# Products of the recurrent half's output projection issued one by one instead of in groups

## The chip, the cores and the metric

The kernel runs on one core of one Trainium2 chip. The metric is the device time of one execution in microseconds (us); lower is better. The engines are named as in the profile: PE is TensorE (matmuls), PEld its weight loads, DVE is VectorE, ACT is ScalarE, POOL is GpSimd, SP is SyncE, which issues all transfers here. Every engine works through its own queue strictly in program order and waits on semaphores for the others.

## The reference, cut to what matters

Two layers run over 512 tokens of width 1024. Layer 1 has a recurrent mixer (a diagonal state-space part and a gated DeltaNet of 6 heads) and then a convolutional FFN. The change lies where layer 1's mixer ends and its FFN begins.

```python
def recurrent_mixer(h, w_in, ...):
    u, q, k, v, z, a, beta_raw = split_cols(h @ w_in, REC_SPLITS)
    yc = s5_mixer(u, ...)                                  # 256 columns
    yd = gated_deltanet_mixer(q, k, v, z, a, beta_raw, ...)  # 6 heads x 128
    return jnp.concatenate([yc, yd], axis=-1) @ w_out      # the output projection

x = x + g1 * recurrent_mixer(modulate(x, norm_mix, sh1, sc1), ...)
h = modulate(x, norm_ffn, sh2, sc2)                        # RMS norm, scale, shift
x = x + g2 * conv_ffn(h, w_up, conv_w, w_down)
```

The delta rule solves a triangular system per chunk and head, then steps through the chunks with a state S that each chunk hands to the next.

## The kernel before

Everything is stored transposed: 8 tiles of 128 channels x 512 tokens. A float32 product is made from three passes (`mm3`): each operand is split into a high and a low part (`hh`/`hl` for activations, `whi`/`wlo` for weights), and high x high, high x low and low x high are accumulated in one PSUM bank. In the trace these are rows of L393 and L394.

**Weights.** `prep` loads a 512 KB weight tile (`st`), ScalarE casts it to `whi` (L363) and VectorE subtracts to make `wlo` (L364). There are two `st` buffers and five `whi`/`wlo` pairs, so a later tile's cast waits until an earlier product has let its pair go.

**The solve and scan.** The DeltaNet heads go in pairs (0, 1, 2). For each pair, `levels` inverts the triangular blocks in small matmuls (L1356, L1363, L1374, L1381, L1384, L1393, L1398, in this order) with a VectorE or ScalarE copy between any two of them. `scan` then makes four chunk steps for both heads: W times the right side (L1414), the state update (L1421), the next chunk's right side (L1409) and the outputs (L1429, L1430), again each waiting for a copy. After the last step come squares on ScalarE (L1443), an inverse root on VectorE (L421 to L426), the gated output `vs` (L1450), eight transposes (L1453) and a copy (L1456), whose result is split into the last two of the eight operand pairs of the output projection (`REC_K` puts them at the end of its sum).

**The output projection.** `out_gemm` makes 8 output tiles m. Tiles 0 to 3 go to the banks acc, acc, t and x over all 512 tokens, as 24 products each of 128x512. For tiles 0 and 1 the last of the eight operand pairs is a part of its own. Tiles 4 to 7 go to s, s, o and o in two halves of 256 tokens, 24 products of 128x256 for each tile and half. After each half of the tokens `norm` follows: a sum over channels (L520), an inverse root on VectorE (L421 to L426), its spread over partitions (L530), and `make_h` (L549 to L551), which writes that half of the FFN's input. The FFN's first four up products also run half by half; then come its tiles in o, o, t and x, and from L626 on the fast scheme `seven`.

**What sets the order.** The program is written once, and a list scheduler lays out each engine's queue before the run, by priorities that follow the written order; work whose inputs are late falls behind ready work. `gemm` hands its products to `runs`, which cuts them into groups of 12 (24 for the 256-token halves). What `together` does with a group depends on one flag:

```python
if not self.grouped:
    for c in calls:
        c()
    return
first = calls[0]()
with self.tc.issue_after(first.ins), self.tc.high_priority(offset=URGENT):
    for c in calls[1:]:
        c()
```

With the flag on, once the first product of a group is placed, the other 11 or 23 get a priority 4000 higher. The flag is off during the recurrent mixer itself and on elsewhere.

Of the kernel before, what the change touches and what calls it, by code (L numbers as in the profile page):

```python
# [249 lines left out]
class Kernel:  # L250
# [887 lines left out]
    def recurrent(self):  # L1138
# [456 lines left out]
        for n in REC_K[len(SPLIT_AT):]:  # L1595
            self.split(Y[n], *rhs[n], half=n < 2)
        self.close("rt")
        self.grouped = True
        self.xp = self.open("x2", "right")
        self.x = [self.xp.tile([P, T], F32, name=f"x{k}") for k in range(KD)]  # L1600
        for k in range(KD):
# [2 lines left out]
        self.keep, self.keep_pool = {}, self.open("fg1", "right")  # L1604
        self.out_gemm([("ro", m) for m in range(8)], rhs, lambda m: self.gate(1, 0, m), 1, 1, hC, REC_K, ("acc", "acc", "t", "x", "s", "s", "o", "o"))
        self.close("hB")

    def build(self):
        nc, I = self.nc, self.I
# [87 lines left out]
```

## Time and profile before

| | us |
|---|---|
| median of 3 runs | 1303.36 |
| the runs | 1301.78, 1303.36, 1312.18 |
| profiled execution, its own time | 1304.43 |
| its span, first to last instruction | 1302.6 |
| PE busy in the span | 1269.6 (97%) |
| DVE busy | 1006.7 (77%) |
| ACT busy | 632.1 (49%) |

A busy PE here is one with a matmul in flight, at whatever clock. The time outside the span is 1.8 us. The stretch that the change touches lies between 868 us, where the solve of pair 2 begins, and 1016 us, a little into the FFN of layer 1.

### The profile page before, as it was taken

What the parts mean: (1) busy time and instruction counts of PE and PEld (TensorE: products, weight loads), DVE (VectorE), ACT (ScalarE), POOL (GpSimd) and SP (SyncE); (2) the same over time, 40 slices, a digit from 0 to 9 for tenths busy, and PEclk for the clock granted to TensorE, in tenths of its full rate; (3) what the DMA queues carried; (4) which work ended last, traced back from release to release, by engine and by line L of the source; (5) the groups of instructions that cost most, each with busy time, mean ns of one, the idle gap of its engine ahead of it and who ended that gap; (6) DMA issues with size and microseconds to landing.
All of it is one profiled execution on the core that took longest, in us unless ns stands there. A gap on an engine that the chain in (4) does not pass through costs nothing.

```text
span 1302.6 us, 22709 instructions
## 1 busy us (share of the span) xinstructions
PE 1269.6 (97%) x8814; PEld 1084.2 (83%) x8814; DVE 1006.7 (77%) x2195; ACT 632.1 (49%) x1214; POOL 12.5 (1%) x43
## 2 busy tenths in 40 slices
PE   8999999999999999999999999998899999999998
PEld 5988776998888888788988878786888999998998
DVE  6868886779995996696779686763679999888883
ACT  4466655445422432243374656552455656554550
POOL 0001000000000000000000000000000000000000
PEclk9999999999999999999999999999999999999999
DMA  9624544516664765473325332220412333332222
GB/s 367 227 84 151 180 153 147 207 46 232 209 198 166 241 227 198 130 239 133 126 102 155 121 97 59 85 62 13 169 47 98 105 102 102 102 102 100 96 84 103
DMA packets 83132, 181.14 MB, mean 139 GB/s; under 512 B 28560, under 2 KB 36176, under 8 KB 83024
## 3 DMA queue, kind: packets, MB, share of 16 engines
q1 hardware_dynamic: 83024, 179.69, 41.1%
q8 instruction: 69, 1.13, 0.4%
q14 instruction: 39, 0.32, 0.1%
HBM read 165.55 MB, written 14.11 MB: 138 GB/s over the span
## 4 chain that ended last, share of the span: by engine, by line
PE 80%; DVE 12%; ACT 4%; DMA 2%; issue 2%; SPq 0%; DVEq 0%; ACTq 0%
PE acc L393 20%; PE acc L394 10%; PE s L393 9%; PE o L393 8%; PE s L394 4%; PE o L394 4%; PE s L626 3%; PE o L626 3%; PE acc L626 2%; PE s L806 2%; PE o L841 1%; DVE wlo L364 1%; DMA st<-up 1%; PE x L393 1%; DVE wlo L332 1%
## 5 line engine op out<-in xcount | busy, mean ns | idle before, releaser
L363 ACT CAST whi<-st 128x1024 fp32r<-128x1024 f32 (+3 forms) x168 | 165.2, 986 | 217.0 <-PE acc L393 68.1
L364 DVE TENSOR_TENSOR wlo<-st,whi 128x1024 fp32r<-128x1024 f32 (+3 forms) x168 | 191.2, 1140 | 47.1 <-ACT whi L363 45.4
L393 PE MATMUL acc<-hh,whi 128*128 128x512 f32 (+1 forms) x392 | 141.5, 368 | 4.2 <-ACT hh L550 3.9
L393 PE MATMUL acc<-hl,whi 128*128 128x512 f32 (+1 forms) x392 | 141.3, 364 | 0.2 <-DVE hl L414 0.2
L394 PE MATMUL acc<-hh,wlo 128*128 128x512 f32 (+1 forms) x392 | 141.2, 363 | 0.0
L465 DVE CUSTOM_DVE_ANT_0 adaj<-ast,cond 128x1024 bf16<-128x1024 f32 x86 | 104.8, 1218 | 10.4 <-DMA ast<-ada 10.2
L393 PE MATMUL acc<-whi,hh 128*128 128x256 f32 x320 | 92.9, 291 | 0.4 <-ACT hh L550 0.4
L394 PE MATMUL acc<-whi,hl 128*128 128x256 f32 x320 | 90.4, 283 | 0.9 <-DVE hl L551 0.9
L393 PE MATMUL acc<-wlo,hh 128*128 128x256 f32 x320 | 90.4, 283 | 0.0
L393 PEld LDWEIGHTS acc<-hh,whi 128*128 128x128 f32 x392 | 73.4, 190 | 17.1 <-ACT hh L550 4.6
L393 PE MATMUL s<-hl,whi 128*128 128x512 f32 (+2 forms) x256 | 86.3, 340 | 0.0
L393 PE MATMUL s<-hh,whi 128*128 128x512 f32 (+2 forms) x256 | 85.8, 344 | 0.0
L393 PEld LDWEIGHTS acc<-hl,whi 128*128 128x128 f32 x392 | 74.0, 190 | 12.3 <-DVE hl L414 0.8
L394 PEld LDWEIGHTS acc<-hh,wlo 128*128 128x128 f32 x392 | 74.3, 190 | 11.1
L394 PE MATMUL s<-hh,wlo 128*128 128x512 f32 (+2 forms) x256 | 82.2, 339 | 0.0
L331 ACT CAST whi<-st 128x1024 fp32r<-128x1024 f32 x54 | 56.3, 1048 | 27.4 <-DVE st L340 7.8
L393 PE MATMUL o<-hh,whi 128*128 128x512 f32 (+1 forms) x192 | 68.8, 358 | 0.0
L332 DVE TENSOR_TENSOR wlo<-st,whi 128x1024 fp32r<-128x1024 f32 x54 | 65.5, 1216 | 4.1 <-ACT whi L331 4.1
L393 PE MATMUL o<-hl,whi 128*128 128x512 f32 (+1 forms) x192 | 68.5, 357 | 0.0
L394 PE MATMUL o<-hh,wlo 128*128 128x512 f32 (+1 forms) x192 | 68.5, 357 | 0.0
L393 PEld LDWEIGHTS acc<-whi,hh 128*128 128x128 f32 x320 | 60.2, 188 | 5.9 <-issue 4.0
L394 PEld LDWEIGHTS acc<-whi,hl 128*128 128x128 f32 x320 | 60.2, 188 | 1.9 <-DVE hl L551 1.5
(909 smaller groups left out, 3473.2 us busy)
## 6 DMA issues: line engine op xcount, KB each, us to landing
ast<-ada SPq DMA_DIRECT2D x92, 512.0 KB
st<-up SPq DMA_DIRECT2D x88, 512.0 KB
st<-ri SPq DMA_DIRECT2D x20, 512.0 KB
st<-wq SPq DMA_DIRECT2D x17, 512.0 KB
st<-dn SPq DMA_DIRECT2D x16, 448.0 KB
st<-dn SPq DMA_DIRECT2D x16, 384.0 KB
st<-dn SPq DMA_DIRECT2D x16, 320.0 KB
st<-wo SPq DMA_DIRECT2D x8, 512.0 KB
```

The costliest lines, as they stand in the source:

```text
L331: nc.scalar.copy(hi, src)
L332: nc.vector.tensor_tensor(lo, src, hi.bitcast(F32), ALU.subtract)
L363: nc.scalar.copy(hi, st)
L364: nc.vector.tensor_tensor(lo, st, hi.bitcast(F32), ALU.subtract)
L393: return [lambda: mm(out, lh, rh, start=start, stop=False), lambda: mm(out, lh, rl, start=False, stop=False), lambda: mm(out, ll, rh, star ...
L394: lambda: mm(out, ll, rh, start=False, stop=stop)]
L465: self.nc.vector.tensor_tensor_reduce(junk, st, self.cond, 1.0, 0.0, op0=ALU.mult, op1=ALU.add, accum_out=self.md[l][:, i:i + 1])
L626: nc.tensor.matmul(acc, x[:, s], y, start=start and k == n == 0, stop=k == 3 and n == 2, skip_group_check=not start)
L806: self.together([lambda sb=sb, pr=pr: nc.tensor.matmul(sb, qT[pr, i * P:(i + 1) * P], kT[pr, j0 * P:(i + 1) * P], start=True, stop=True) f ...
L841: calls.append(lambda j=j, par=par, vc=vc: nc.tensor.matmul(ob[64 * par:64 * par + 64, i * P:(i + 1) * P], V[:, j0 + j, vc:vc + 64], pts[: ...
```

## The change

The line that turns the flag on again moves from in front of the output projection to behind it. So the eight tiles' products, the last pair's solve and scan, and the two halves of the norm are all laid out with one product at a time to place. Nothing is added or removed; the same instructions run in another order.

```diff
         self.close("rt")
-        self.grouped = True
         self.xp = self.open("x2", "right")
 ...
         self.out_gemm([("ro", m) for m in range(8)], rhs, lambda m: self.gate(1, 0, m), 1, 1, hC, REC_K, ("acc", "acc", "t", "x", "s", "s", "o", "o"))
         self.close("hB")
+        self.grouped = True
```

The first place is TensorE in the solve of pair 2, from L1384 on. Names are out<-in with tile names; `acc` is tile 0 or 1 of the projection and `t` tile 2. Before:

```order
L1384 MATMUL s<-iW,z 32x32 x16
L393 MATMUL acc<-hh_9711,whi 128x512
L393 MATMUL acc<-hl_9712,whi 128x512
L394 MATMUL acc<-hh_9711,wlo 128x512
L393 MATMUL acc<-hh_9713,whi 128x512
L393 MATMUL acc<-hl_9714,whi 128x512
L394 MATMUL acc<-hh_9713,wlo 128x512
L1393 MATMUL s<-x_6823,nq 64x64 x8
```

With the change, TensorE at the same place:

```order
L1384 MATMUL s<-iW,z 32x32 x16
L393 MATMUL acc<-hh_9715,whi 128x512
L393 MATMUL acc<-hl_9716,whi 128x512
L394 MATMUL acc<-hh_9715,wlo 128x512
L1393 MATMUL s<-x_6823,nq 64x64 x8
L393 MATMUL acc<-hh_9717,whi 128x512
L393 MATMUL acc<-hl_9718,whi 128x512
L394 MATMUL acc<-hh_9717,wlo 128x512
L1398 MATMUL s<-wf,x_6823 64x64 x8
```

Three products stand between two steps of the solve where 6 or 12 stood.

The second place is TensorE at the end of pair 2's scan, where L1430 writes the last outputs and L1453 transposes the gated result. Before:

```order
L1421 MATMUL s<-vk,kt 128x128
L1430 MATMUL o<-vn,nq 128x128 x2
L1409 MATMUL s<-St,kT 128x128
L1429 MATMUL o<-St,qd 128x128
L1414 MATMUL s<-rh,wf 128x128
L1430 MATMUL o<-vn,nq 128x128
L1453 MATMUL s<-ident,vs 128x128 x7
L393 MATMUL s<-hh_9711,whi 128x256
L393 MATMUL s<-hl_9712,whi 128x256
```

With the change, TensorE from the last L1414 on:

```order
L1414 MATMUL s<-rh,wf 128x128
L393 MATMUL t<-hl_9716,whi 128x512
L1430 MATMUL o<-vn,nq 128x128
L394 MATMUL t<-hh_9715,wlo 128x512
L1430 MATMUL o<-vn,nq 128x128
L393 MATMUL t<-hh_9717,whi 128x512
L393 MATMUL t<-hl_9718,whi 128x512
L394 MATMUL t<-hh_9717,wlo 128x512
```

Behind the last L1430 now stand 19 products of tiles 2 and 3 (t and x) before the first L1453, and single products between the transposes; before, nothing stood between the two.

The third place is TensorE around the first half's norm, where L520 sums over channels and L530 spreads the inverse root. Before:

```order
L393 MATMUL o<-hl_9726,whi 128x256
L394 MATMUL o<-hh_9725,wlo 128x256
L530 MATMUL t<-ident,nry 128x128 x2
L520 MATMUL x<-ones,stat 128x1 x2
L393 MATMUL acc<-hh_10048,whi 128x256 x2
L393 MATMUL s<-hh_10048,whi 128x256 x2
```

With the change, TensorE around the same L530:

```order
L393 MATMUL s<-hh_9723,whi 128x256
L393 MATMUL s<-hl_9724,whi 128x256
L530 MATMUL t<-ident,nry 128x128 x2
L394 MATMUL s<-hh_9723,wlo 128x256
L393 MATMUL s<-hh_9725,whi 128x256
L393 MATMUL s<-hl_9726,whi 128x256
```

The first L530 used to stand behind the whole projection; now 52 of its products, all of the second half of the tokens, stand behind it and 31 between it and its L520. The second half's L520 and L530 stand 48 and 72 products into the FFN's first up products, where before the first half's L530 and the second half's L520 stood next to each other.

## Rows read from the trace of the kernel before

**Rows 1.** Busy time by stretch: from:to, length, busy us of each engine, PEclk, DMA.

```profile
846.00:860.00 14.00, 14.00 (x115) 13.32 (x114) 10.70 (x39) 5.81 (x20) 0.00 (x0) 1.00 0.30 65
...
903.00:910.00 7.00, 2.82 (x10) 1.87 (x11) 4.20 (x21) 2.15 (x10) 0.00 (x0) 0.75 0.00 0
910.00:914.00 4.00, 4.00 (x12) 3.14 (x12) 0.69 (x1) 0.29 (x1) 0.00 (x0) 0.59 0.88 266
...
947.00:951.00 4.00, 4.00 (x22) 3.90 (x21) 4.00 (x11) 1.90 (x5) 0.00 (x0) 0.57 0.49 186
...
963.00:995.00 32.00, 32.00 (x185) 28.09 (x184) 31.18 (x57) 22.65 (x38) 0.00 (x0) 1.00 0.15 50
```

**Rows 2.** Timeline of PE, pair 1: start, us, instruction, idle before and releaser.

```profile
837.58 0.69 PE L1374 MATMUL s<-iX,nq 32*32 32x32 f32 x32
...
845.88 0.38 PE L1414 MATMUL s<-vs,wf 128*128 128x128 f32 x2
...
848.04 0.39 PE L1409 MATMUL s<-St,kT 128*128 128x128 f32 x2
```

**Rows 3.** Timeline of PE, pair 2: solve and scan.

```profile
868.33 0.75 PE L1356 MATMUL s<-iX,nq 32*32 32x32 f32 x64
...
875.37 0.69 PE L1374 MATMUL s<-iX,nq 32*32 32x32 f32 x32
...
888.24 0.61 PE L1414 MATMUL s<-vs,wf 128*128 128x128 f32 x4
...
892.37 0.39 PE L1409 MATMUL s<-St,kT 128*128 128x128 f32 x2
...
893.27 0.43 PE L1414 MATMUL s<-rh,wf 128*128 128x128 f32 x2
...
894.92 0.38 PE L1421 MATMUL s<-vk,kt 128*128 128x128 f32 x2
...
903.09 0.49 PE L1430 MATMUL o<-vn,nq 128*128 128x128 f32 x2 [0.39 <-DVE vn L1419]
```

**Rows 4.** Timeline of PE, from the scan's end to the last operand.

```profile
907.67 2.02 PE L1453 MATMUL s<-ident,vs 128*128 128x128 f32 x7 [4.09 <-DVE vs L1450]
909.69 0.58 PE L393 MATMUL s<-hh,whi 128*128 128x256 f32 x1
...
913.41 0.39 PE L393 MATMUL t<-hl,whi 128*128 128x512 f32 x1
913.64 0.40 PE L393 MATMUL x<-hh,whi 128*128 128x512 f32 x1
...
918.51 0.50 PE L393 MATMUL t<-hh,whi 128*128 128x512 f32 x1 [1.43 <-ACT hh L413]
```

**Rows 5.** Timeline of PE, the two norms and the FFN's first products.

```profile
944.80 0.71 PE L530 MATMUL t<-ident,nry 128*128 128x128 f32 x4 [2.35 <-DVE nry L426]
...
946.63 0.51 PE L393 MATMUL acc<-hh,whi 128*128 128x256 f32 x2 [0.78 <-ACT hh L550]
...
950.90 0.28 PE L393 MATMUL acc<-hh,whi 128*128 128x256 f32 x1
951.02 0.28 PE L393 MATMUL s<-hl,whi 128*128 128x256 f32 x1
...
961.13 0.51 PE L393 MATMUL acc<-hh,whi 128*128 128x256 f32 x2 [1.11 <-ACT hh L550]
```

**Rows 6.** Timeline of PE, the start of the fast scheme.

```profile
994.51 0.28 PE L626 MATMUL acc<-hh,whi 128*128 128x256 f32 x1
...
999.72 0.39 PE L626 MATMUL acc<-b01h,whi 128*128 128x256 f32 x1 [0.96 <-ACT whi L331]
```

**Rows 7.** Timeline of DVE: in the solve, behind the scan, the second norm.

```profile
874.61 0.41 DVE L1365 TENSOR_TENSOR iX<-iX,s 128x256 f32<-128x256 f32 x1
...
907.26 2.16 DVE L1450 SCALAR_TENSOR_TENSOR vs<-o,ory,zg 128x128 f32<-128x128 f32 x8
...
960.05 1.26 DVE L549 SCALAR_TENSOR_TENSOR hk<-x,am,t 128x256 f32<-128x256 f32 x3 [5.93 <-PE t L530]
```

## The prediction, made before the changed kernel ran

> **What bounds the kernel now.** I read the busy times first: TensorE is occupied for 97% of the span, so a change of order can only win what TensorE loses, as waits or at a lower clock, inside the stretch that is reordered. The list of busy time by stretch shows where that is [rows 1]: from 903 to 910 us TensorE is busy for 2.82 of 7 us, and from 910 to 914 and from 947 to 951 it is busy throughout, but at a granted clock of 0.59 and 0.57, close to 1.2 GHz of its two levels (1.2 and 2.4 GHz), each time behind an idle stretch. The timeline of TensorE then gives the single waits: a scan that ends with nothing beside it [rows 3], 4.09 us for the gated output and 1.43 us for the last operand [rows 4], 2.35, 0.78 and 1.11 us around the two norms [rows 5]. Meanwhile products of the projection that depend on none of this are waiting for their turn: their groups were all placed earlier, or can't start before the last operand. Last, VectorE: from 963 to 995 us it is busy for 31.18 of 32 us [rows 1], so the FFN's start is close to a bound of its own.
>
> **The change part by part.** No instruction is added or dropped, so I keep a ledger of TensorE's lost time: what goes, and what comes new. Prices: a 128x512 product follows the next by 0.23 us (913.41 to 913.64) [rows 4], a 128x256 one by 0.12 us (950.90 to 951.02) [rows 5], and a 128x128 matmul of the scan takes 0.225 us (four from 892.37 to 893.27) [rows 3].
>
> What goes:
> - The scan's bare tail. From 894.92 to 903.09 us TensorE runs 22 scan matmuls and no product [rows 3]: 8.17 us for 22 x 0.225 = 4.95 us of work, 3.2 us lost. With the change each step holds three products.
> - The gated output: 4.09 us [rows 4]. Nineteen products of tiles 2 and 3 now stand there, 19 x 0.23 = 4.4 us.
> - Seven transposes take 2.02 us [rows 4], paced by `vs`, of which VectorE writes eight in 2.16 us [rows 7]. A transpose is one pass (x7 for seven) where a scan matmul is two (x2 for one), half of 0.225 us, so 0.8 us of it is work; products now stand between them, and 1.2 us goes.
> - The lower clock behind it: nine products, two of 256 and seven of 512, from 909.69 to 913.41 us [rows 4], 3.72 us for 2 x 0.12 + 7 x 0.23 = 1.85 us of work: 1.9 us.
> - The last operand: 1.43 us [rows 4]. It arrives behind tiles 2 and 3 as before, but earlier against them: five products stand behind the fourth transpose, and tiles 0 to 2 then take it.
> - The norms: 2.35 + 0.78 + 1.11 = 4.2 us [rows 5]. The second half of the tokens (96 products of 0.12 us, 11.5 us) now lies beside the first half's root and input, and the FFN's first products beside the second's.
> - The lower clock behind the first norm: 21 products from 946.63 to 950.90 us [rows 5], 4.27 us for 2.5 us: 1.8 us.
>
> Together 3.2 + 4.1 + 1.2 + 1.9 + 1.4 + 4.2 + 1.8 = 17.8 us.
>
> What comes:
> - The head of the solve. L1374 needs `iX`, which VectorE writes at 874.61 to 875.02 us behind two weight splits that stay in front of it [rows 7]; so L1374 moves only from 875.37 [rows 3] to about 875.1 us. But 12 products (4 and 8) stand before it where 18 did: 6 x 0.23 - 0.3 = 1.1 us is lost.
> - The rest of the solve, L1374 to L1414, was laid out with 3 products at a time for pair 1 already, since the flag is off there. It took 845.88 - 837.58 = 8.30 us [rows 2], with 13 products and four transposes (3.0 + 0.45 us): 4.85 us for steps and hand-overs. Pair 2 took 888.24 - 875.37 = 12.87 us [rows 3] with 36 products (8.3 us): 4.6 us. The change has 15 products there, 3.45 + 4.85 = 8.3 us; 0.25 us more of hand-overs.
> - The scan: L1414 to L1409 takes 848.04 - 845.88 = 2.16 us in pair 1 [rows 2], L1409 to the next L1414 893.27 - 892.37 = 0.90 us [rows 3], so 3.06 us a step, for ten matmuls and three products (2.25 + 0.69 = 2.94 us). Three steps lose 0.4 us, the last one, with two single products inside, about 0.5 us: 0.9 us. The scan then ends near 875.1 + 8.3 + 3 x 3.06 + 1.5 = 894 us, 9 us earlier, and the first transpose comes near 899 us.
> - The norms that stay: 31 products (3.7 us) stand between the first half's L520 and L530, 24 (2.9 us) between the second's. The trace has no norm with so much beside it. The bounds are 0 and the old 2.35 + 1.11 us; I take 0.8 us, near the lower end, because the old waits had no product beside them at all.
> - The start of the fast scheme. TensorE waits 0.96 us there for a cast weight [rows 6], which comes behind VectorE's queue. VectorE's part moves with the second norm too (its first `hk` at 960.05 us waits for L530) [rows 7], so I expect about the same wait and put 0.5 us more; bounds -0.96 us (the wait goes) and +4 us (VectorE, full from 963 us on, can't follow).
>
> Together 1.1 + 0.25 + 0.9 + 0.8 + 0.5 = 3.5 us. Net gain 17.8 - 3.5 = 14.3 us. From the profiled execution's 1304.43 us this gives 1290.1 us; its own run was 1.07 us above the median of 1303.36 us, so against the median I predict **1289.1 us**. A short way into the fast scheme all queues have the old order again, so a shift there is kept to the end.
>
> One price could turn this around. TensorE's granted clock was 1.00 all through 846 to 860 us [rows 1], which is pair 1's scan with single products and short gaps, the pattern that the change spreads to pair 2. The Trainium skill, on its page "TensorE: Matmul & The Clock Gate", section "A second HAM failure mode: psum-queue depth-cycling", reports a kernel in which short idles between matmul groups, with the PSUM banks taken in turn, made the clock swing between its two levels and cost throughput. By this rule the reordered stretch would lose more than it wins (the second rival below gives the price); by the row it loses nothing, and the sum above goes by the row.
>
> **The rivals.**
> 1. VectorE takes part of it back. The second norm and the split of the next weights share VectorE's queue. If the second half's chain stays bare (its 1.11 us, the first's 2.35 and 0.78 us, and the slow 1.8 us behind an idle, 6.0 us in all) and the fast scheme starts late by up to 2 us more, the gain is 14.3 - 6.0 - 2 = 6.3 us, or 1297 us. For it: 31.18 of 32 us [rows 1]. Against it: VectorE's 5.93 us of idle in front of the second `hk` [rows 7], time that its queue has to spare.
> 2. Slower: the clock. If single products between steps let the granted clock fall to 1.2 GHz at the solve, it would return only with the unbroken products near 899 us. The stretch holds 58 products and 34 scan matmuls; a slow one costs twice as much [rows 4], so 58 x 0.23 + 34 x 0.225 = 21 us more, a net 6.7 us slower, 1310 us. It decides once more than 14.3 of the 21 us are lost, about two thirds of the stretch at the lower level. The skill's page named above speaks for it; the 1.00 in pair 1's scan [rows 1] speaks against it.
> 3. More: the waits at the norms vanish altogether and the FFN's 0.96 us too, with its own dip of the clock: 17.8 - 2.2 + 3 = 18.6 us, 1284.8 us.
> 4. It moves nothing: the gaps in the queue are filled, but weights come no earlier, and the FFN's start, held by transfers and casts, stays where it is. The order speaks against it: the casts of up weights wait for buffers that the projection's products let go, and these come earlier too. Within 2 us of 1303 us.
>
> **How the numbers follow.** About 1% (13 us) is what a measurement of this kernel tells from no change. The forecast (gain of 10 to 17 us) gets 0.66, rival 1 0.18, rival 2 0.05, rival 3 0.07 and rival 4 0.04. The range of 1284 to 1298 us holds the forecast, rival 3 and most of rival 1, and leaves out rivals 2 and 4 and the rest. Faster by over 1% means below 1290.3 us: rival 3 whole and 0.8 of the forecast, whose middle lies 1.3 us inside and whose new terms I have taken rather high; 0.07 + 0.53 = 0.60. Slower by over 1% is 0.03 (only rival 2, and only if the low clock lasts beyond the scan), and within 1% the rest, 0.37.
>
> **What the profile will show.** L1414 of the second chunk step of pair 2 near 886 us and the last L1430 near 894 us; no idle in front of the first L1453, which comes near 899 us and is followed by single products; clock 1.00 from 868 to 940 us; the first half's L530 near 927 us and the second's near 943 us (before, the first stood at 944.80 us, and the `hk` behind the second at 960.05 us), with no wait over 1 us at either; the first L626 near 980 us. The prediction is wrong if the clock dips inside the scan, if L1430 ends after 898 us, or if the wait at L626's weights grows by several us.

## The result, and the profile after

The changed kernel takes 1285.45 us (median of 4 runs, 1285.31 to 1287.63) against 1302.62 us for the kernel before (median of 4 runs): ratio 0.9855, 95% interval 0.9816 to 0.9895, or 17.2 us faster. Forecast were 14.3 us and 1289.1 us; the range of 1284 to 1298 us holds the result. Its profiled execution took 1285.57 us, with a span of 1283.8 us, 18.8 us shorter than before.

The list of busy time by stretch, changed kernel; columns as in [rows 1]:

```profile
880.00:894.00 14.00, 14.00 (x103) 12.17 (x104) 7.25 (x22) 3.43 (x12) 0.00 (x0) 1.00 0.00 1
903.00:910.00 7.00, 7.00 (x38) 5.76 (x37) 5.33 (x8) 3.30 (x5) 0.00 (x0) 1.00 0.98 319
910.00:914.00 4.00, 4.00 (x36) 4.00 (x35) 2.77 (x5) 2.48 (x4) 0.00 (x0) 1.00 0.42 149
947.00:951.00 4.00, 4.00 (x35) 3.94 (x34) 3.90 (x12) 4.00 (x9) 0.00 (x0) 1.00 0.02 4
963.00:995.00 32.00, 32.00 (x207) 29.14 (x206) 31.40 (x45) 21.31 (x34) 0.00 (x0) 1.00 0.30 100
```

TensorE has no idle time left in these stretches, and the granted clock is 1.00 in all of them, in the scan (880 to 894 us) too; the 0.59 and 0.57 of before [rows 1] are gone. VectorE is as full as before from 963 to 995 us. The timeline of TensorE in the changed kernel, solve, scan and transposes (answers to [rows 3, 4]):

```profile
866.83 0.75 PE L1356 MATMUL s<-iX,nq 32*32 32x32 f32 x64
...
869.79 0.72 PE L1363 MATMUL s<-iW,z 32*32 32x32 f32 x62 [0.58 <-DVE z L1358]
...
872.06 0.26 PE L1363 MATMUL s<-z,iW 32*32 32x32 f32 x5 [1.03 <-issue]
...
874.30 0.69 PE L1374 MATMUL s<-iX,nq 32*32 32x32 f32 x32
...
882.70 0.38 PE L1414 MATMUL s<-vs,wf 128*128 128x128 f32 x2
...
885.76 0.43 PE L1414 MATMUL s<-rh,wf 128*128 128x128 f32 x2
...
893.55 0.38 PE L1430 MATMUL o<-vn,nq 128*128 128x128 f32 x2
898.55 0.33 PE L1453 MATMUL s<-ident,vs 128*128 128x128 f32 x1 [0.18 <-DVE vs L1450]
```

The 4.09 us in front of the first transpose have become 0.18 us. The same view, the two norms and the start of the fast scheme (answers to [rows 5, 6]):

```profile
921.61 0.61 PE L520 MATMUL x<-ones,stat 128*128 128x1 f32 x4
...
925.99 0.71 PE L530 MATMUL t<-ident,nry 128*128 128x128 f32 x4
...
938.33 0.50 PE L520 MATMUL x<-ones,stat 128*128 128x1 f32 x4
...
941.60 0.60 PE L530 MATMUL t<-ident,nry 128*128 128x128 f32 x4
...
978.55 0.28 PE L626 MATMUL acc<-hh,whi 128*128 128x256 f32 x1
...
979.97 0.28 PE L626 MATMUL acc<-b00h,whi 128*128 128x256 f32 x1
...
982.12 0.39 PE L626 MATMUL acc<-b01h,whi 128*128 128x256 f32 x1
...
1002.24 0.39 PE L626 MATMUL x<-b00h,wlo 128*128 128x256 f32 x1 [0.41 <-DVE wlo L332]
```

No wait stands at any of the norms' four rows, nor between them, and the 0.96 us in front of the `b01h` row of L626 [rows 6] is gone too. The last row, with a wait of 0.4 to 0.5 us that every version has, serves as a mark below. The same view of the kernel before, for the second L530, the first `b00h` row, the second wait at L626 (the first is in [rows 6]) and the mark:

```profile
959.41 0.60 PE L530 MATMUL t<-ident,nry 128*128 128x128 f32 x4
...
995.87 0.28 PE L626 MATMUL acc<-b00h,whi 128*128 128x256 f32 x1
...
1000.66 0.39 PE L626 MATMUL s<-hh,whi 128*128 128x256 f32 x1 [0.44 <-ACT whi L331]
...
1021.44 0.39 PE L626 MATMUL x<-b00h,wlo 128*128 128x256 f32 x1 [0.39 <-DVE wlo L332]
```

Where the 18.8 us of span lie, from such rows of the two traces:

| piece of the trace | before, us | after, us | gain |
|---|---|---|---|
| start to L1356 of pair 2 (same order in both) | 868.33 | 866.83 | 1.50 |
| L1356 to L1374 | 7.04 | 7.47 | -0.43 |
| L1374 to the first L1414 | 12.87 | 8.40 | 4.47 |
| first L1414 to the last L1430 | 14.85 | 10.85 | 4.00 |
| last L1430 to the first L626 | 91.42 | 85.00 | 6.42 |
| first L626 to the mark at `x<-b00h,wlo` | 26.93 | 23.69 | 3.24 |
| mark to the end of the span | 281.16 | 281.56 | -0.40 |

The first line is no effect of the change; from L1356 to the end the span is 434.27 us before and 416.97 us after, 17.3 us less, which is what the medians say. Up to the first L626 the gain is 14.46 us. With 1.5 us added for the first line, the rows foretold near 886, 894, 899, 927, 943 and 980 us stand at 887.3, 895.1, 900.1, 927.5, 943.1 and 980.1 us: the scan some 1 us late, the norms and L626 where they were expected. The ledger without its last term gave 17.8 - 1.1 - 0.25 - 0.9 - 0.8 = 14.75 us. The missing 3 us lie at the fast scheme's start.

### The profile page after: what moved, and what is told of

It reads as the page before. It is cut to its first block, busy times and chain, and to the rows that moved or that the text cites. A ratio compares the mean times of both kernels' runs of the same rounds, so it can differ in the third digit from the quotient of the medians.

```text
span 1283.8 us, 22712 instructions
## 1 busy us (share of the span) xinstructions
PE 1262.4 (98%) x8814; PEld 1079.6 (84%) x8814; DVE 1007.7 (78%) x2195; ACT 632.2 (49%) x1214; POOL 12.3 (1%) x43
## 4 chain that ended last, share of the span: by engine, by line
PE 83%; DVE 9%; DMA 3%; ACT 3%; issue 1%; SPq 0%; DVEq 0%; ACTq 0%
PE acc L393 20%; PE acc L394 10%; PE s L393 10%; PE o L393 9%; PE s L394 5%; PE o L394 5%; PE s L626 3%; PE o L626 2%; PE acc L626 2%; PE s L806 2%; PE o L841 2%; PE x L393 1%; DVE wlo L332 1%; DMA st<-up 1%; DVE adaj L465 1%
## 5 line engine op out<-in xcount | busy, mean ns | idle before, releaser
L364 DVE TENSOR_TENSOR wlo<-st,whi 128x1024 fp32r<-128x1024 f32 (+3 forms) x168 | 191.2, 1140 | 47.2 <-ACT whi L363 45.0
L393 PEld LDWEIGHTS acc<-wlo,hh 128*128 128x128 f32 x320 | 60.5, 189 | 1.6 <-issue 1.6
```

Of the source, the lines that this page charges most:

```text
L364: nc.vector.tensor_tensor(lo, st, hi.bitcast(F32), ALU.subtract)
L393: return [lambda: mm(out, lh, rh, start=start, stop=False), lambda: mm(out, lh, rl, start=False, stop=False), lambda: mm(out, ll, rh, star ...
```

## The experiments

Theory H: the FFN's start was won by a head start. The second L530 went forward from 96 to 72 products into the FFN, VectorE's queue behind it went forward against TensorE's products, and so the casts that L626 waits for are in time. Rival B: the weights' casts came earlier because the projection's products let their buffers go earlier, and VectorE's work is hidden. Of the other terms, the theories are those of the prediction. The chips of these runs differed by some us in stretches that no edit touches, the kernel before took 1307.2 us beside the first four, 1305.6 us beside the next four and 1307.3 us beside the last two, so besides the ratios (each against the kernel before on the same chip) I compare times from L1356 of pair 2 to the mark: 153.11 us before, 135.41 us after. These come from one profiled execution of each kernel; the changed kernel's two differ by 0.25 us. Edits add lines, so L626 is L627 or L628 in some of the kernels.

**Half the change: tiles 0 to 3.**

```diff
+        self.grouped = True
         w = [self.weight(keys[m]) for m in range(4, 8)]
```

> Single products for tiles 0 to 3, groups again from tile 4 on. Order: solve, scan and transposes as in the changed kernel; both norms have products beside them (48 and 24), but the second L530 stands behind the FFN's first 96 up products again, as in the kernel before, not behind 72. Theory H (head start): the 3.2 us that the FFN's start won came because the second L530, and with it VectorE's queue, went forward by 24 products; then the 1.1 us at the second norm's input, the wait at L626's weights (0.96 and 0.44 us) and the low clock behind it come back, 1285.4 + 1.1 + 3.2 = 1289.7 us. Rival B (buffers): the weights come earlier because the projection's products let their buffers go earlier; no wait at L626, 1285.4 + 1.1 = 1286.5 us. Either way the clock is 1.00 from 868 to 940 us and L1430 ends near 894 us.

Measured: ratio 0.9871 (0.9847 to 0.9894); L1356 to the mark 138.92 us, 3.5 us behind the changed kernel. Its timeline of TensorE, from the second L530 on:

```profile
945.76 0.60 PE L530 MATMUL t<-ident,nry 128*128 128x128 f32 x4
947.49 0.50 PE L393 MATMUL acc<-hh,whi 128*128 128x256 f32 x2 [1.11 <-ACT hh L550]
...
982.24 0.28 PE L627 MATMUL acc<-b00h,whi 128*128 128x256 f32 x1
...
986.08 0.39 PE L627 MATMUL acc<-b01h,whi 128*128 128x256 f32 x1 [0.96 <-ACT whi L331]
987.02 0.39 PE L627 MATMUL s<-hh,whi 128*128 128x256 f32 x1 [0.44 <-ACT whi L331]
```

All three waits of before are back to the hundredth, with the second L530 behind 96 products again, as H says. B isn't out yet: the products of tiles 4 to 7, which let buffers go as well, are in groups again too. From L530 to the `b01h` row it takes 986.08 - 945.76 = 40.32 us, before 999.72 - 959.41 = 40.31 us: the length of the chain through VectorE. In the changed kernel TensorE itself comes to that row 982.12 - 941.60 = 40.52 us behind L530, without a wait; the cast that the row needs starts at 981.01 us and takes some 1.0 us, so it ends less than 0.1 us ahead. The two are in balance, with next to nothing to spare.

**The other half: tiles 4 to 7.**

```diff
+        last, self.grouped = not self.grouped, True
         for m0 in range(0, 4, 2):
 ...
+        self.grouped = not last
         w = [self.weight(keys[m]) for m in range(4, 8)]
```

> The other half alone: groups for tiles 0 to 3, single products for tiles 4 to 7. Order: solve and scan as in the kernel before (22 bare scan matmuls, no product between the last scan step and the transposes), norms as in the changed kernel, second L530 behind 72 up products. The ledger's terms of the norms (2.35 + 0.78 + 1.11 + 1.8 us of low clock) go, those of the scan (3.2, 4.1, 1.2, 1.9 us) stay. Theory H: the FFN's start wins 3.2 us too, 1302.6 - 6.0 - 3.2 = 1293.4 us. Rival B: the weights' buffers are let go as late as before against VectorE, the wait at L626 stays, 1302.6 - 6.0 = 1296.6 us.

Measured: ratio 0.9909 (0.9885 to 0.9934), L1356 to the mark 141.85 us, 11.26 us better than before. TensorE in this kernel:

```profile
907.24 2.02 PE L1455 MATMUL s<-ident,vs 128*128 128x128 f32 x7 [4.09 <-DVE vs L1452]
...
949.50 0.60 PE L530 MATMUL t<-ident,nry 128*128 128x128 f32 x4
...
987.47 0.28 PE L628 MATMUL acc<-b00h,whi 128*128 128x256 f32 x1
...
989.62 0.39 PE L628 MATMUL acc<-b01h,whi 128*128 128x256 f32 x1
```

The scan's losses stand as before (4.09 us), those of the norms and of L626 are gone. H asked for 9.2 us; the rest is mostly the 1.43 us for the last operand, which this order spares too. So the two halves of the change are worth some 11 us for tiles 4 to 7 and 14 us for tiles 0 to 3 alone (153.11 - 138.92), and 17.7 us together. Of the 7.7 us that they share, 6.3 us are accounted for: both cure the first norm (4.9 us) and the last operand (1.4 us).

**VectorE given more to do.**

```diff
-            V_.tensor_tensor(a, h[:, t1], h[:, t2], ALU.subtract)
+            for _ in range(3):
+                V_.tensor_tensor(a, h[:, t1], h[:, t2], ALU.subtract)
```

> The changed kernel, and VectorE writes each of four token sums (L601, 0.34 us from start to start) three times instead of once: 8 x 0.34 = 2.7 us more work for VectorE between the second norm and the fast scheme, and nothing else. Theory H (the FFN's start was won by VectorE's head start): L530 to the first L626 of the fast scheme was 38.4 us without the waits and 36.5 us with them; 2.7 us more work is like 35.7 us, so the waits at L626's weights come back, 1.4 us and up to 0.8 us more, with the low clock behind them: 3 to 5 us slower than the changed kernel. Rival B (buffers and transfers set the casts' time): VectorE's work is hidden, within 0.5 us of the changed kernel, and no wait there.

Measured: ratio 0.9899 (0.9878 to 0.9919), the changed kernel beside it 0.9862 (0.9843 to 0.9882); L1356 to the mark 139.17 against 135.16 us, 4.0 us more. TensorE:

```profile
980.18 0.28 PE L627 MATMUL acc<-b00h,whi 128*128 128x256 f32 x1
...
982.48 0.39 PE L627 MATMUL acc<-b00h,wlo 128*128 128x256 f32 x1 [0.50 <-DVE wlo L332]
...
985.26 0.39 PE L627 MATMUL acc<-b01h,whi 128*128 128x256 f32 x1 [1.33 <-ACT whi L331]
986.21 0.38 PE L627 MATMUL s<-hh,whi 128*128 128x256 f32 x1 [0.44 <-ACT whi L331]
```

Nothing but VectorE's work was added, and the waits are there, 2.27 us of them, with the clock at 0.74 from 985 to 990 us. B, by which this work is hidden, falls.

**The changed kernel again**, beside the last one:

> The changed kernel once more, as the base for the three beside it. All theories: from L1356 of pair 2 to the span's end some 417 us (before: 434 us), no wait in front of L626's first weights, ratio near 0.987. What it tells is how much of the difference to other runs arises outside of the reordered stretch.

Measured: as just given; L1356 stands at 868.53 us, where before's trace had it (868.33), and L1356 to the end is 417.57 us. So the 1.5 us in front of L1356 in the first comparison was of that execution alone.

**Is the low clock the price of the idle stretch?** The kernel before, with five filler matmuls in front of the transposes:

```diff
                 b = self.bank("s")
+                if p == 2 and n == 0:
+                    with self.tc.issue_after(self.mm.ins):
+                        for _ in range(5):
+                            M_.matmul(b, self.ident, d["qd"], start=True, stop=True)
```

(`self.mm` is the last L1430; the line that sets it is left out here.)

> The kernel before, with five matmuls of 128x512 float32 (0.59 us each, 3.0 us) put on TensorE behind the last L1430, into the bank that the transposes overwrite; nothing reads them. VectorE's chain to the gated output is as long as before, so TensorE can start the transposes no earlier. Theory C (the low clock from 910 to 914 us is the price of the idle stretch): the clock stays at 1.00 there, and the transposes and products behind them win 1.9 us and some 0.5 us of the transposes: 2 to 2.5 us faster than before. Rival: the clock is low there for what the products do (the weights' transfers and splits start at the same time), and it stays near 0.59: no difference.

Measured: ratio 0.9994 (0.9977 to 1.0011), no difference that can be told; L1356 to the mark 151.12 us, 2.0 us less than before. Busy time by stretch, this kernel:

```profile
907.00:910.00 3.00, 3.00 (x11) 1.29 (x10) 2.63 (x11) 0.85 (x2) 0.00 (x0) 1.00 0.00 0
910.00:914.00 4.00, 4.00 (x22) 3.36 (x23) 0.69 (x1) 0.46 (x1) 0.00 (x0) 1.00 0.77 246
945.00:950.00 5.00, 4.84 (x22) 4.85 (x23) 4.88 (x14) 2.89 (x8) 0.00 (x0) 0.50 0.47 188
1000.00:1005.00 5.00, 4.56 (x37) 4.37 (x37) 5.00 (x7) 3.25 (x6) 0.00 (x0) 1.00 0.40 114
```

And the kernel before in the last two of these stretches:

```profile
945.00:950.00 5.00, 4.22 (x25) 4.04 (x25) 4.53 (x13) 2.62 (x6) 0.00 (x0) 0.74 0.71 256
1000.00:1005.00 5.00, 4.56 (x26) 4.22 (x26) 5.00 (x6) 2.78 (x5) 0.00 (x0) 0.70 0.35 111
```

The fillers take 4.4 us, and the first transpose starts 4.62 us behind the last L1430 as against 4.58 us before, so the wait is only filled, not shortened. With work in the idle stretch the clock stays at 1.00 behind it, with weights being loaded there as before (DMA 0.77 and 0.88): theory C. The first L530 comes 1.8 us earlier (74.70 instead of 76.47 us behind L1356), the 1.9 us of the ledger. Some of it is lost at the first norm, where the same wait (2.35 us) is followed by a deeper dip (from the first to the second L530 it takes 15.9 us here and 14.6 us before), and won again at L626, where the same waits (0.96 and 0.44 us) cost no clock at all this time.

**Smaller groups.** The kernel before with groups of 6 in this projection:

```diff
+        self.run = 6
         self.out_gemm([("ro", m) for m in range(8)], rhs, ...
```

> The kernel before with groups of 6 (12 in the halves) in this projection. Order: the first two scan steps have 6 products each, the last ones 6 too (36 products from the first L1414 to the last L1430), but no product stands in front of the seven transposes, and the second L520 and L530 stand side by side behind the FFN's 96 products. The ledger by its terms: of the scan's bare tail 3.2 us goes, the 4.1, 1.2 and 1.9 us around the transposes stay; the first norm's 2.35 + 0.78 + 1.8 us go (48 products stand beside it), and the same three come new at the second norm, with its old 1.11 us; the FFN's start keeps its wait. Net 3.2 us and the head of the solve as in the change: 2 to 3 us faster than before. A rival, that the gain grows with the number of pieces: half of 17 us.

Measured: ratio 0.9985 (0.9966 to 1.0003), no difference that can be told; L1356 to the mark 149.46 us, 3.65 us better than before. TensorE:

```profile
904.50 2.02 PE L1453 MATMUL s<-ident,vs 128*128 128x128 f32 x7 [4.09 <-DVE vs L1450]
...
953.43 1.19 PE L530 MATMUL t<-ident,nry 128*128 128x128 f32 x4 [2.51 <-DVE nry L426]
```

The wait at the transposes is untouched, and the bare norm has moved from the first half to the second, as the order says. By these two traces half the group size gives a fifth of the gain: what counts is whether a product is left in front of each wait.

**More of the same: groups off through the FFN's first four up products.**

```diff
+            self.grouped = True
             for j in range(NJ):
 ...
-        self.grouped = True
         self.xp = self.open("x2", "right")
```

(The edit is shown against the kernel before; the loop over `j` begins behind the FFN's first four up products.)

> Groups stay off through the FFN's first four up products too: the second L530 moves forward by 9 products more. Theory H: the changed kernel has no wait left at L626's first weights, so a longer head start of VectorE buys nothing there, at most the waits of 0.41, 0.28 and 0.38 us further on: 1284.5 to 1285.5 us. A rival: VectorE still sets the pace from 980 us on, and each 0.12 us of head start is time: 9 x 0.12 = 1.1 us, 1284.3 us, with the three waits gone.

Measured: ratio 0.9865 (0.9829 to 0.9901); L1356 to the mark 134.73 us, 0.4 to 0.7 us less than the two traces of the changed kernel; the small waits at the mark and behind it stay (0.43, 0.24, 0.37 us), and the second L530 now waits for 0.28 us. The rival's 1.1 us is not there: once the chain through VectorE is covered, more head start is worth next to nothing. Its trace also shows the head of the solve without the 1.03 us of "issue":

```profile
870.82 0.71 PE L1364 MATMUL s<-z,iW 32*32 32x32 f32 x62
...
874.11 0.69 PE L1375 MATMUL s<-iX,nq 32*32 32x32 f32 x32 [0.53 <-DVE iX L1366]
```

L1374 (here L1375) waits for `iX` and comes 6.84 us behind L1356; 6.77 us were forecast.

**Groups off everywhere**, by `if True:` for `if not self.grouped:`.

> No groups anywhere, in layer 0 too. TensorE is idle there for 2.7 us from 100 to 300 us and 1.0 us from 600 to 700 us, so if single products fill idle time as they did beside the scan, up to 3.7 us go: 1282 us. The rival: groups earn something there (they keep a bank's products together, so that the copy out of it can start and the bank comes free), and single products let several banks fill side by side: 1288 us or more, with new waits of TensorE on banks.

Measured: ratio 0.9990 (0.9974 to 1.0007). From L1356 to the mark it is the changed kernel (135.41 us), but L1356 stands at 883.40 us: layer 0 has lost some 15 us. The transposes of the attention's last head groups, changed kernel and then this one:

```profile
196.25 0.66 PE L829 MATMUL t<-ident,S 128*128 128x128 f32 x4 [0.56 <-ACT qT L763]
```

```profile
207.68 0.55 PE L829 MATMUL t<-ident,S 128*128 128x128 f32 x3 [0.56 <-ACT qT L763]
```

11.4 us are lost by there, and not as idle time: TensorE is busy for 49.94 of 50 us from 150 to 200 us. Nor is it more work or a lower clock: up to these rows both kernels run 1410 matmuls, at a clock of 1.00. But the same small matmuls of the attention take longer: the 176 of L841 are busy for 22.1 us instead of 15.9, the 64 of L806 on `kTa` for 15.5 instead of 12.7, together 9.0 of the 11.4 us. They stand between single products there; that this alone makes them longer was not tried.

**Layer 0's projections too.** First only their last four tiles (attention and FFN down), then the whole of the attention's, each on top of the changed kernel:

```diff
+        self.grouped = False
         w = [self.weight(keys[m]) for m in range(4, 8)]
```

(The lines that turn the flag on again are left out. This one stands in the function that all output projections share, so the last four tiles of layer 1's FFN down product, near the end of the kernel, are issued one by one too, which the expectation does not count.)

> The changed kernel, and in layer 0's two output projections (attention, FFN down) the last four tiles, in halves of 256 tokens, are issued one by one too; their first four stay in groups. TensorE's waits at layer 0's norms in the changed kernel: 1.11 us before the FFN's second half (272 us), and 0.94 us of idle time from 600 to 650 us. Theory (single products belong where a norm's chain would stand bare): up to 2.0 us faster than the changed kernel, 1283.4 us where that took 1285.4 us. A rival: the norm of layer 0 had other work beside it already (mixed groups of the next projection), so the 1.11 us only turn into more passes of small matmuls between products: no difference.

```diff
+            self.grouped = False
             self.out_gemm([("wo", m) for m in range(8)], ...
+            self.grouped = True
```

> The changed kernel, and the whole of the attention's output projection is issued one by one, its first four tiles beside the last heads of the attention too. The norm wins 1.1 us as in the run beside it. Where all groups were off (the run before with no groups anywhere), layer 0 lost 15 us up to L1356 of pair 2; if that came from single products between the attention's small matmuls in general, some of it shows here: 2 to 5 us slower than the changed kernel at the first L530 of layer 0. Rival: the loss came from the attention's own projections; then this is 1 us faster than the changed kernel.

Measured: ratios 0.9850 (0.9834 to 0.9867) and 0.9857 (0.9842 to 0.9872), neither apart from the changed kernel's 0.9862. The wait in question, in the first of the two:

```profile
272.88 0.50 PE L393 MATMUL acc<-hh,whi 128*128 128x256 f32 x2 [1.11 <-ACT hh L550]
```

It is 1.11 us as in the changed kernel: the FFN's up products are in groups there, and by the order the second L530 stands behind all of the first half's. Neither expectation of a gain came true, and the 2 to 5 us of loss didn't either, so what is left for the 11.4 us of the run without any groups is the attention's own projections, which were not tried alone. No version beats the changed kernel by more than the measurement can tell.

## Where the prediction was right, and where it was wrong

- **What goes, 17.8 us:** right. The rows of the waits are gone, the clock is 1.00 throughout, and the sum up to the first L626 is 14.46 us where the ledger has 14.75 us. That the sum fits so well is partly luck: the head of the solve came out 0.7 us worse and the norms 0.8 us better. That the low clock follows the idle stretch was shown by the filler matmuls for the first dip (1.8 us of its 1.9 us); for the dip at the norm it was not tried.
- **The head of the solve, 1.1 us:** too low in this execution. L1374 came 7.47 us behind L1356 instead of 6.77, with 6 products (1.38 us) fewer in between: 1.8 us. The trace puts 1.03 us of it down to "issue" in the middle of L1363; in three of the other traces, with the same order, L1374 comes at 6.83 to 6.84 us, and the term is 1.2 us; in four more it comes at 7.13 to 7.21 us, again with such a gap.
- **The rest of the solve and the scan:** right; 8.40 us for 8.3, and 10.85 us for 3 x 3.06 + 1.5 = 10.7.
- **The norms that stay, 0.8 us:** nothing stayed; the lower bound was the right one, but the reason was not. The old waits didn't stand without any product: in the kernel before, 24 products stand between the first L520 (939.00 us) and its L530 (944.80 us), 5.80 us apart, and the wait of 2.35 us comes behind all of them. What made that chain long were two weight splits (L364) between its steps in VectorE's queue. VectorE in the kernel before, then in the changed kernel at the second norm:

```profile
939.60 0.15 DVE L525 TENSOR_SCALAR nv<-x 128x2 f32<-128x2 f32 x1
...
941.73 1.23 DVE L364 TENSOR_TENSOR wlo<-st,whi 128x1024 fp32r<-128x1024 f32 x1
...
943.45 1.22 DVE L364 TENSOR_TENSOR wlo<-st,whi 128x1024 fp32r<-128x1024 f32 x1
944.59 0.15 DVE L426 SCALAR_TENSOR_TENSOR nry<-nrt,nry 128x2 f32<-128x2 f32 x1
```

```profile
938.87 0.16 DVE L525 TENSOR_SCALAR nv<-x 128x2 f32<-128x2 f32 x1 [1.02 <-PE x L520]
...
941.04 0.16 DVE L426 SCALAR_TENSOR_TENSOR nry<-nrt,nry 128x2 f32<-128x2 f32 x1
...
942.61 1.26 DVE L549 SCALAR_TENSOR_TENSOR hk<-x,am,t 128x256 f32<-128x256 f32 x3
```

The chain takes 5.14 us with two splits in it and 2.33 us with none (3.68 us with one, at the changed kernel's first norm). So 31 products (4.38 us from L520 to L530) and 24 (3.27 us) covered it; with two splits in it neither would have. The first rival named such splits as a risk; the forecast itself did not count them, and that they lie elsewhere in the new order was its luck.
- **The start of the fast scheme, 0.5 us lost:** this is the step that failed. I took it that "VectorE's part moves with the second norm too" and expected "about the same wait". It moved further: `hk` of the second norm went from 960.05 us [rows 7] to 942.61 us, 17.4 us, where the first L626 went 16.0 us. The change puts the second L530 at 72 products into the FFN instead of 96, and those 24 products (2.9 us), less the 1.11 us of wait that went, are VectorE's head start: 1.8 us by the count, 1.5 us by the two rows, where 0.96 and 0.44 us were needed. The order told it before the run: I had counted where L530 stands, and did not weigh it against the FFN's products, which are what VectorE's work has to keep up with. Put at a loss of 0.5 us, the term measured 3.24 us won: 1.40 us of waits, some 1.5 us of lower clock behind them (0.70 from 1000 to 1005 us before; the kernel with the filler matmuls has the same waits at 1.00 and takes 25.39 us for the piece that took 26.93), and 0.3 us that I can't place. With it the gain of 17.2 us ended just above the 10 to 17 us that the forecast stood for.
- **The rivals.** The fourth, that nothing moves, and the first, VectorE taking it back, did not come; VectorE was nearly the bound, though: 2.7 us of extra work cost 4.0 us. The second, a falling clock, did not come either: 1.00 from 880 to 894 us with single products. TensorE is busy for 14.00 of 14 us there, and so it was from 846 to 860 us [rows 1]; the "short gaps" that I read into that row are not in it. Short idles stand in the bare scan of the kernel before: from 895 to 903.6 us TensorE is busy for 7.31 of 8.6 us, with waits of 0.22 and 0.39 us, at a clock of 1.00. The Trainium skill, on its page "TensorE: Matmul & The Clock Gate", section "A second HAM failure mode: psum-queue depth-cycling", has a kernel in which frequent short idles between groups of matmuls made the clock swing. The scan of before does not show that swing within its 8.6 us, and the changed kernel, without such idles, does not test it. The third, with 18.6 us, is what happened but for the head of the solve: the waits at the norms and at L626 went, with the dip behind them. It had 0.07 against the forecast's 0.66, so the case that came was one held unlikely. That the kernel gets faster by over 1%, which it did, had 0.60.

## What to carry to other kernels

Grouping products costs where the groups swallow what could stand beside a chain of small steps: count, in each engine's order, how many products stand in front of every wait, and size the gain by the waits that get one. When a step moves, measure its move against the work of the engine that will later need its result, not against the wall clock: here VectorE's work came 17.4 us earlier by the wall clock and 1.5 us earlier against TensorE's products. Look into the queue of the engine that runs the chain too: two weight splits between its steps made a wait of 2.35 us. A low clock behind an idle stretch can be part of the price of the wait: in the kernel before, some 5.2 us (1.9, 1.8 and 1.5) behind 9.7 us of waits at the transposes, the norms and L626.

## What I had not expected of the hardware

- The same waits don't always bring the same clock. At L626, 0.96 and 0.44 us of waiting came with 0.70 in 1000 to 1005 us before, and with 1.00 in the kernel with the filler matmuls; and from the first to the second L530, with the same 2.35 us in front, that kernel took 1.3 us longer. What decides it was not tried.
- An "issue" gap in the middle of L1363's small matmuls (1.03 us after; 0.76 us in the kernel with single products for tiles 0 to 3 alone) comes in some executions of the same order and is absent in others, so a term of 1 us in such a place can't be read from one trace.
- Single products made the attention of layer 0 11.4 us longer without more idle time of TensorE, more matmuls or a lower clock: matmuls of L841 and L806 between them took 9.0 us more. Beside the solve and scan of pair 2 single products cost no such time (8.40 us for the 8.3 us forecast, and 10.85 us for 10.7 us).
